# An encoder layer on one core: SBUF tiles moved to addresses that are multiples of 128 bytes

## The chip, the cores and the metric

One core of a Trainium2 chip runs the whole layer. The metric is the device time of one execution in microseconds (us). The kernel before takes 878.75 us, the median of 3 runs (878.52 to 878.77).

## What is computed

One encoder layer on x (512 positions, 1024 channels), all in float32. A projection by `w_in` feeds eight heads of differential attention and a Mamba-2 scan in both directions with 16 heads in 4 groups. The two results, side by side, go through `w_out`; then come a layer norm, SwiGLU (22 column tiles of 128) and a second layer norm:

```
h   = x @ w_in                                  # q, k, v | z, x/B/C, dt
a   = softmax(q1 k1 - |i-j| slope) - lam * softmax(q2 k2 - |i-j| slope)
att = rmsnorm(a @ v) * subln_w * (1 - lambda_init)
ssd = rmsnorm_grouped((scan_fwd + scan_bwd + D x) * silu(z)) * norm_w
x   = layernorm(alpha * x + [att, ssd] @ w_out)
x   = layernorm(alpha * x + (silu(x @ w_gate) * (x @ w_up)) @ w_down)
```

## The kernel before

A float32 product is made of three products in float32r, a float32 format that TensorE takes in one pass. Every operand is split into a high part h and a low part l, and `mm3` (L174 to L179) adds h·h, h·l and l·h. ScalarE makes h by a copy and VectorE makes l by a subtraction (L106 and L107 for the weights). The small products (transposes, attention times v, the scan's products) stay in float32.

```
174    def mm3(o, pairs, first=True, last=True):
177            T.matmul(o, ah, bh, start=first and i == 0, stop=False)
178            T.matmul(o, ah, bl, start=False, stop=False)
179            T.matmul(o, al, bh, start=False, stop=last and i == n - 1)
```

In a matmul the first operand (`ah`) is the stationary one, which the engine loads ahead (LDWEIGHTS, the rows PEld), and the second (`bh`) is the moving one, which streams through, one column of the result for each of its columns. In the profile's names it is out<-moving,stationary: in `wo<-wh,mixl` the weights `wh` move and `mixl` stands.

The stages, in order of time. The first 250 us project B, C, x and z for one scan group after another (`col_units` L181 with 512 moving columns, `row_units` L196 with 256) and run the scan steps of the group before between them (L398 to L518). Then come eight heads of attention (L574 to L645), woven with the next heads' projections q, k (512 columns) and v (256 columns). From about 445 us the output projection runs (`wo`, 512 columns, `outer_units` L650 and `tile_major` L764; the last four weight chunks are kept in tiles `hold`), then the first layer norm. SwiGLU (L946 to L997) multiplies by Winograd's 2 x 2 form: seven products of 256 columns for each column tile, made by `product` (L882 to L889). Two of them take the split weights `wh`, `wl` as the stationary operand, five take sums of weight blocks or a split block (`S1` to `S4`, `A22`), which VectorE makes (L815, L854). The down projection (`dn`, L1006 to L1059) has 512 moving columns again, with the last chunks in tiles `keep` and the last bank in two halves of 256 columns (`dn13`).

The order on each engine is the order of the code with the scheduler's lookahead; nothing in it depends on where a tile lies. A tile's place in SBUF comes from its pool. Pools stack up from the left end, or from the right end with `side="right"`, and every tile's size is rounded up to 32 bytes a partition. So the tiles of 420, 16, 8 and 4 bytes in the first pool (L85 to L90), `msk` with 3920 bytes (L123), and the small tiles of the scan, the heads and the norms push all that lies behind them off any larger grid. The addresses that the program gets, taken modulo 128:

```
 0: cst (with the identity); sx, xd, h, L, yy, gg and the rest of the scan's pool
64: rE, co_B, co_x, co_C, dts, ex, wd, wdp, xraw
96: wr, wh, wl, xh, xl (later x1h, x1l, keep), QS, KS, kl, va, mixh, mixl, msk,
    T1 to T4, lhsC, hid, the ring of split hid tiles (tiles 1 to 9)
32: ss, as, hold, S1 to S4, A22, the resident split hid tiles (10 to 21)
```

Slices within a tile begin at multiples of 128 bytes in all large products but those of `rE`, whose runs are 256 bytes long. The right end of SBUF that the pools are given lies at 96 modulo 128.

Of the kernel before, what the change touches and what calls it, by code (L numbers as in the profile page):

```python
# [8 lines left out]
F32 = mybir.dt.float32  # L9
# [4 lines left out]
P = 128  # L14
NWARM = 2
S = 512
NT = 4
# [25 lines left out]
M_LE, M_GE, M_GT, M_LT, M_ONE, M_HM, M_RM, M_SEL, M_TRI, N_M = 0, 128, 256, 384, 512, 640, 656, 660, 916, 980  # L43
N_C = 1024

V_BIAS, V_ALOG, V_DSK, V_LAM, N_V = 0, 32, 64, 80, 336
P_CW, P_CB, P_SUB, P_NW, N_P = 0, 80, 96, 97, 105
# [3 lines left out]
def encoder(ctx, tc, xt, xs, wall, wdt, consts, masks, vecs, pvec, lnv, out):  # L51
    nc = tc.nc
    V, A, G, T = nc.vector, nc.scalar, nc.gpsimd, nc.tensor
# [19 lines left out]
    def weave(steps, units, counts):  # L73
        """Emits steps in order with counts[i] of the units after step i, and the remaining units at the end."""
        done = 0
        for f, n in zip(steps, counts, strict=True):
            f()
            for u in units[done:done + n]:
                u()
            done += n  # L80
        for u in units[done:]:
            u()

# [1 line left out]
    cst = cp.tile([P, N_C], F32, name="cst")  # L85
    vec = cp.tile([P, N_V], F32, name="vec")
    pv = cp.tile([P, N_P], F32, name="pv")
    mhalf = cp.tile([P, 4], F32, name="mhalf")
    lam = cp.tile([P, 2], F32, name="lam")
    nlam = cp.tile([P, 1], F32, name="nlam")  # L90
    V.memset(mhalf, -0.5)
# [23 lines left out]

# [1 line left out]
    xh = xtp.tile([P, KT, S], R32, tag="xh", name="xh")  # L117
# [4 lines left out]
    ep = eps_.enter_context(tc.tile_pool(name="ep", bufs=1))  # L122
    msk = ep.tile([P, N_M], F32, name="msk")  # L123
    with tc.tile_pool(name="xraw", bufs=1) as xr:
# [56 lines left out]
    def col_units(i, name, done, step=2):  # L181
        """x @ w for 128 columns, transposed: [columns, 512]; then done(psum)."""
        st = {}
# [12 lines left out]
    def row_units(i, name, tag, done):  # L196
        """x @ w for 256 columns: two banks of [128 positions, 2, 256]; done(half, psum)."""
        st = {}
# [16 lines left out]

# [1 line left out]
    sps = ExitStack()  # L217
# [25 lines left out]
    co = {}  # L243
    first_units = conv_units(0, sp, co)

# [1 line left out]
    dtv = ep.tile([P, 2, NT, NH], F32, name="dtv")  # L247
# [4 lines left out]
    sel = msk[:, M_SEL:M_SEL + 256].rearrange("p (a k) -> p a k", a=2)  # L252
    # per direction d: rows erow[d] carry the exponents, the other 64 rows the mask
    erow = (slice(0, 64), slice(64, 128))
# [115 lines left out]

    # stationary parts of the exponents per direction and half of the columns, in the last mix tiles' places
    lhsC = [[mxp[0].tile([P, NT, P], R32, tag=f"m{q}{14 + d}", name=f"lhsC{d}{q}") for q in "hl"] for d in range(2)]
# [6 lines left out]

    # mix^T in two float32r parts: 16 tiles of [128 channels, 512]  # L380
    mixh, mixl = [None] * 16, [None] * 16
# [6 lines left out]

# [1 line left out]
    bc = lambda a, n: a[:, :, None].broadcast_to([a.shape[0], 4, n])  # L390
# [3 lines left out]
    def scan_steps(g):  # L394
        cT, bT, x0, x1 = (co[k, g] for k in ("C", "B", "x0", "x1"))
        sx, H, Ms, yb, gg = {}, {}, {}, {}, {}
        szs = {}
        ssq = sp.tile([P, NT], F32, tag="ssq", name=f"ssq{g}")  # L398
        gs = slice(4 * g, 4 * g + 4)
# [115 lines left out]

# [1 line left out]
    va, qk = {}, {}  # L517
# [31 lines left out]

# [1 line left out]
    late = []  # L551
# [18 lines left out]

# [1 line left out]
    mxp[0] = mxs.enter_context(tc.tile_pool(name="mxa", bufs=1, side="right"))  # L572

    def head_steps(h, ap):  # L574
        QS, KS, kl = qk[h]
        vv, j = va[h // 2], h % 2
        tab = ap.tile([P, 896], F32, tag="tab", name=f"tab{h}")
        mn = ap.tile([P, NT, 2], F32, tag="mn", name=f"mn{h}")
        Z = ap.tile([P, NT, 2], F32, tag="Z", name=f"Z{h}")
        rz = ap.tile([P, NT, 2], F32, tag="rz", name=f"rz{h}")  # L580
        co_ = ap.tile([P, NT], F32, tag="co", name=f"co{h}")
        oq = ap.tile([P, NT], F32, tag="oq", name=f"oq{h}")
        ss, ats, st = {}, {}, {}
# [39 lines left out]
        def fin():  # L623
            f = ap.tile([P, NT], F32, tag="f", name=f"f{h}")
            V.tensor_tensor(f, rz[:, :, 0], rz[:, :, 0], op=ALU.mult)
# [19 lines left out]

# [1 line left out]
    def pair(i, ahead=None):  # L647
        return [w.rearrange("p (k c) -> p k c", k=2) for w in wget(i, ahead)]

    def outer_units(i0, order, lhs, acc, n0, n1, total):  # L650
        """acc(t) += lhs tiles (pairs in order) x weight chunks i0 + n0 .. i0 + n1 - 1."""
        st = {}
# [46 lines left out]

# [1 line left out]
    fx = ctx.enter_context(tc.tile_pool(name="fx", bufs=1))  # L701
# [10 lines left out]
    st6 = fx.tile([P, NT, 4, 6], F32, name="st6")  # L712
    rs = fx.tile([P, NT, 1], F32, name="rs")
    mv = fx.tile([P, NT, 2], F32, name="mv")

# [48 lines left out]
    def tile_major(i0, order, lhs, acc, done, hold, after):  # L764
        """As outer_units, with the last NHELD chunks resident and used one sequence tile at a time."""
        n = len(order)
# [28 lines left out]

# [1 line left out]
    hidp = ctx.enter_context(tc.tile_pool(name="hid", bufs=1, side="right"))  # L797
# [11 lines left out]

    # Winograd's 2 x 2 form: operands from x1^T's blocks B (k half, sequence half)  # L810
    def block(i, j):
# [16 lines left out]
    def t_steps(q):  # L828
        """x1^T of sequence tile 2 + q, and the operands that come of it."""
        b12, b22 = x1t(2 + q, 0), x1t(2 + q, 1)  # L830
# [12 lines left out]

    # operands from the weight blocks of two column tiles: A11 A12 / A21 A22 (columns, k half)
    ops, mats = {}, {}
# [50 lines left out]
    def put(j, f, c, src):  # L896
        """One block of gate (silu) or up (times gate) into hid."""
        d = hid_tile(f)[:, c]
        if j % 2 == 0:
            A.activation(d, src, AF.Silu)  # L900
        else:
            V.tensor_tensor(d, d, src, op=ALU.mult)
# [42 lines left out]

    # the first two tiles of gate and up, whole; sequence half 0 of three chunks first  # L946
    def ff_w(f, w):
# [50 lines left out]

# [1 line left out]
    NEARLY = 1  # L1000
# [5 lines left out]
    def hid_split(e, ph):  # L1006
        """hid tile e in two parts; the later tiles' parts stay for both column halves."""
        key = e if e >= NRING else (ph, e)
# [136 lines left out]
```

## Time and profile before

| | |
|---|---|
| median of 3 runs | 878.75 us |
| span of the profiled execution, first to last instruction | 876.8 us |
| TensorE (PE) busy | 862.4 us, 98% of the span |
| weight loads (PEld) busy | 748.6 us, 85% |
| VectorE (DVE) busy | 616.6 us, 70% |
| ScalarE (ACT) busy | 457.7 us, 52% |
| GpSimd (POOL) busy | 121.3 us, 14% |

The profiled execution's own device time is not given apart from its span; the median of the runs is 1.95 us above the span. In a matmul's row the duration is longer than what it costs, because matmuls are pipelined: the next one starts while the last results still drain. What a matmul costs in a stream is the distance from its start to the next start, called its pitch here. It is read from the timeline.

### The profile page before, as it was taken

How to read it: one execution, taken by the hardware profiler on the slowest of the kernel's cores; microseconds unless marked ns; L12 is line 12 of the kernel's file. 1: busy time of each engine (PE TensorE's matmuls, PEld its weight loads, DVE VectorE, ACT ScalarE, POOL GpSimd, SP SyncE). 2: the span in 40 equal slices, each digit the busy share in tenths (PEclk: the TensorE clock that was granted, in tenths of full speed). 3: DMA queues.
4: the chain of work that ended last, by engine and by line, in shares of the span. 5: the costliest groups of instructions: out<-in, count | busy, mean ns of one | idle time of the engine just before them, and what ended most of it. 6: DMA issues, size and time to landing. Idle time of an engine off the chain costs nothing.

```text
span 876.8 us, 13791 instructions
## 1 busy us (share of the span) xinstructions
PE 862.4 (98%) x5404; PEld 748.6 (85%) x5404; DVE 616.6 (70%) x1071; ACT 457.7 (52%) x893; POOL 121.3 (14%) x137
## 2 busy tenths in 40 slices
PE   7999999999999999999999999999999999999996
PEld 3888989899778687786788889999999999888885
DVE  4978788786567666766644579988888887733617
ACT  4777776667456555655632314555555555621500
POOL 3025252535400000000000023000000000000002
PEclk9999999999999999999999999999999999999999
DMA  7321212112212103111135600343233233332402
GB/s 259 113 96 49 73 50 80 66 49 70 76 49 72 50 25 96 50 49 49 49 109 186 209 25 25 112 129 98 96 123 118 98 116 133 112 96 96 145 1 96
DMA packets 23008, 78.74 MB, mean 90 GB/s; under 512 B 2688, under 2 KB 2944, under 8 KB 22944
## 3 DMA queue, kind: packets, MB, share of 16 engines
q1 hardware_dynamic: 22320, 75.60, 25.8%
q0 software_dynamic: 624, 2.27, 0.8%
q8 instruction: 42, 0.69, 0.3%
q14 instruction: 22, 0.18, 0.1%
HBM read 75.77 MB, written 2.10 MB: 89 GB/s over the span
## 4 chain that ended last, share of the span: by engine, by line
PE 67%; DVE 4%; ACT 1%; issue 1%; DMA 0%; POOLq 0%; POOL 0%; DVEq 0%; ACTq 0%
PE M L887 12%; PE N L887 6%; PE dn L178 4%; PE dn L177 4%; PE dn L179 4%; PE wo L177 3%; PE wo L178 3%; PE wo L179 3%; PE C L887 3%; PE o L618 3%; PE s L592 2%; PE s L590 2%; PE at L606 1%; PE v L177 1%; PE k L177 1%; PE q L177 1%
## 5 line engine op out<-in xcount | busy, mean ns | idle before, releaser
L107 DVE TENSOR_TENSOR wl<-wr,wh 128x1024 fp32r<-128x1024 f32 x101 | 124.5, 1233 | 66.8 <-ACT wh L106 63.5
L106 ACT CAST wh<-wr 128x1024 fp32r<-128x1024 f32 x101 | 105.7, 1049 | 77.6 <-PE wo L179 28.6
L598 ACT ACTIVATE ss<-ss,mn 128x512 f32<-128x512 f32 x64 | 46.0, 720 | 25.9 <-DVE mn L595 25.8
L595 DVE CUSTOM_DVE_ANT_0 ss<-s,tab 128x512 f32<-128x512 f32 x64 | 43.2, 688 | 16.4 <-PE s L592 15.8
L178 PE MATMUL dn<-wl,hidh 128*128 128x512 f32 x130 | 51.0, 392 | 0.0
L177 PE MATMUL dn<-wh,hidh 128*128 128x512 f32 x130 | 50.9, 392 | 0.0
L179 PE MATMUL dn<-wh,hidl 128*128 128x512 f32 x130 | 50.6, 389 | 0.0
L893 ACT COPY e<-M 128x256 f32<-128x256 f32 x60 | 22.4, 372 | 43.1 <-PE M L887 43.0
L456 ACT ACTIVATE rE<-vals,msk 64x128 fp32r<-64x128 f32 x128 | 43.0, 391 | 1.0 <-DVE vals L339 0.4
L177 PE MATMUL wo<-wh,mixh 128*128 128x512 f32 x96 | 38.3, 399 | 0.0
L177 PE MATMUL v<-wh,xh 128*128 128x256 f32 x128 | 37.8, 296 | 0.0
L178 PE MATMUL wo<-wl,mixh 128*128 128x512 f32 x96 | 37.6, 392 | 0.0
L179 PE MATMUL wo<-wh,mixl 128*128 128x512 f32 x96 | 37.5, 390 | 0.0
L179 PE MATMUL v<-wh,xl 128*128 128x256 f32 x128 | 36.7, 286 | 0.0
L177 PE MATMUL z<-wh,xh 128*128 128x256 f32 x128 | 36.4, 286 | 0.0
L178 PE MATMUL v<-wl,xh 128*128 128x256 f32 x128 | 36.3, 284 | 0.0
L179 PE MATMUL z<-wh,xl 128*128 128x256 f32 x128 | 36.2, 283 | 0.0
L178 PE MATMUL z<-wl,xh 128*128 128x256 f32 x128 | 36.2, 283 | 0.0
L618 PE MATMUL o<-va,as 128*128 128x128 f32 x256 | 34.0, 275 | 0.1
L724 POOL TENSOR_TENSOR rs<-rs,mhalf 128x1 f32<-128x1 f32 x8 | 12.2, 1525 | 158.6 <-DVE rs L723 158.6
L708 POOL DMA_DIRECT2D ln<-in_lnv x4 | 2.3, 580 | 227.1 <-PE dn L178 208.8
L618 PEld LDWEIGHTS o<-va,as 128*128 128x128 f32 x256 | 31.6, 192 | 0.7 <-ACT osq L621 0.3
(355 smaller groups left out, 2926.6 us busy)
## 6 DMA issues: line engine op xcount, KB each, us to landing
wr<-in_wall SPq DMA_DIRECT2D x130, 512.0 KB, 3.5
xraw<-in_xt SPq DMA_DIRECT2D x8, 256.0 KB, 6.8
xr<-in_xs SPq DMA_DIRECT2D x4, 512.0 KB, 6.3
ln<-in_lnv POOLq DMA_DIRECT2D x4, 512.0 KB, 4.4
out_y<-xr SPq DMA_DIRECT2D x8, 256.0 KB, 2.0
msk<-in_masks SPq DMA_DIRECT2D x1, 490.0 KB, 5.7
cst<-in_consts SPq DMA_DIRECT2D x1, 448.0 KB, 6.7
vec<-in_vecs POOLq DMA_DIRECT2D x1, 168.0 KB, 5.9
```

The lines of the kernel that those rows point to most:

```text
L106: A.copy(h, raw)
L107: V.tensor_tensor(l, raw, h.bitcast(F32), op=ALU.subtract)
L177: T.matmul(o, ah, bh, start=first and i == 0, stop=False)
L178: T.matmul(o, ah, bl, start=False, stop=False)
L179: T.matmul(o, al, bh, start=False, stop=last and i == n - 1)
L456: A.activation(r[d][e, h], vals[e, sls[t]], AF.Copy, scale=hmask[e, 4 * g + h:4 * g + h + 1])
L590: T.matmul(sbs[c], QS[:, c, sl], KS[:, c], start=True, stop=False)
L595: V.tensor_tensor_reduce(out=s, in0=sb, in1=tab[:, 384 - 128 * t:896 - 128 * t], scale=1.0, scalar=3.0e38, op0=ALU.add, op1=ALU.min, accum ...
L598: A.activation(s, s, AF.Exp, scale=-1.0, bias=mn[:, t, c:c + 1], accum_out=Z[:, t, c:c + 1])
L618: T.matmul(o, ats[t][:, kt * P:(kt + 1) * P], vv[:, kt, j * P:(j + 1) * P], start=kt == 0, stop=kt == NT - 1)
L887: T.matmul(o, x[:, k], y[:, k], start=first and n == 0, stop=last and n == 11, skip_group_check=True)
L893: mats[j]["i" + name] = A.copy(e, src)
```

## The change

The small tiles are merged into few tiles whose sizes are multiples of 128 bytes (`small` with 1792, `msk` with 3968, `sm` with 256 for each head, `rsmv` with 128), the scan's `ssq` moves into spare columns of `msk`, and a tile `top` of 96 bytes is set at the right end. After it every tile that the kernel makes begins at a multiple of 128 bytes.

```diff
-    vec = cp.tile([P, N_V], F32, name="vec")
-    pv = cp.tile([P, N_P], F32, name="pv")
-    mhalf = cp.tile([P, 4], F32, name="mhalf")
-    lam = cp.tile([P, 2], F32, name="lam")
-    nlam = cp.tile([P, 1], F32, name="nlam")
+    small = cp.tile([P, 448], F32, name="small")
+    vec = small[:, 0:N_V]
+    pv = small[:, N_V:N_V + N_P]
+    o_ = N_V + N_P
+    mhalf, lam, nlam = (small[:, o_ + a:o_ + b] for a, b in ((0, 4), (4, 6), (6, 7)))
+    top = ctx.enter_context(tc.tile_pool(name="top", bufs=1, side="right"))
+    top.tile([P, 24], F32, name="top")
...
-    msk = ep.tile([P, N_M], F32, name="msk")
+    mskt = ep.tile([P, 992], F32, name="msk")
+    msk = mskt[:, 0:N_M]
...
-        ssq = sp.tile([P, NT], F32, tag="ssq", name=f"ssq{g}")
+        ssq = mskt[:, N_M + 4 * (g % 2):N_M + 4 * (g % 2) + 4]
...
-        mn = ap.tile([P, NT, 2], F32, tag="mn", name=f"mn{h}")
-        Z = ap.tile([P, NT, 2], F32, tag="Z", name=f"Z{h}")
-        rz = ap.tile([P, NT, 2], F32, tag="rz", name=f"rz{h}")
-        co_ = ap.tile([P, NT], F32, tag="co", name=f"co{h}")
-        oq = ap.tile([P, NT], F32, tag="oq", name=f"oq{h}")
+        sm = ap.tile([P, 64], F32, tag="sm", name=f"sm{h}")
+        mn, Z, rz = (sm[:, 8 * i:8 * i + 8].rearrange("p (t c) -> p t c", c=2) for i in range(3))
+        co_, oq, f = (sm[:, 24 + 4 * i:28 + 4 * i] for i in range(3))
...
-            f = ap.tile([P, NT], F32, tag="f", name=f"f{h}")
...
-    rs = fx.tile([P, NT, 1], F32, name="rs")
-    mv = fx.tile([P, NT, 2], F32, name="mv")
+    rsmv = fx.tile([P, 32], F32, name="rsmv")
+    rs = rsmv[:, 0:NT].rearrange("p (t c) -> p t c", c=1)
+    mv = rsmv[:, NT:3 * NT].rearrange("p (t c) -> p t c", c=2)
```

No instruction is added, removed or moved on any engine; only the tiles' names and addresses differ. One wait is added. On GpSimd, in the heads of attention, the power that ends a head's RMSNorm (L628, on the tile `f`) waits for VectorE before the change:

```order
L628 TENSOR_TENSOR f_3333<-f_3333,mhalf 128x4 [waits DVE_49]
L584 TENSOR_SCALAR tab_3907<-cst 128x896 [waits DVE_49,Pool_49]
L628 TENSOR_TENSOR f_3615<-f_3615,mhalf 128x4 [waits DVE_49]
L584 TENSOR_SCALAR tab_4175<-cst 128x896 [waits DVE_49,Pool_49]
L628 TENSOR_TENSOR f_3870<-f_3870,mhalf 128x4 [waits DVE_49]
```

From the third head on it waits for ScalarE (Activation) too, since `f` now shares the tile `sm` with columns that ScalarE writes:

```order
L629 TENSOR_TENSOR sm_3088<-sm_3088,small 128x4 [waits DVE_49,Activation_49]
L586 TENSOR_SCALAR tab_3878<-cst 128x896 [waits DVE_49,Pool_49]
L629 TENSOR_TENSOR sm_3352<-sm_3352,small 128x4 [waits DVE_49,Activation_49]
L586 TENSOR_SCALAR tab_4141<-cst 128x896 [waits DVE_49,Pool_49]
L629 TENSOR_TENSOR sm_3615<-sm_3615,small 128x4 [waits DVE_49,Activation_49]
```

The instructions and their order are the same; the added wait stands at six of the eight heads.

## Rows read from the trace of the kernel before

**Rows 1.** The page: TensorE's share of the span, and its granted clock in 40 slices.

```profile
PE 862.4 (98%) x5404; PEld 748.6 (85%) x5404; DVE 616.6 (70%) x1071; ACT 457.7 (52%) x893; POOL 121.3 (14%) x137
...
PEclk9999999999999999999999999999999999999999
```

**Rows 2.** Busy time by stage: stretch (us), sum, then each engine with its instructions.

```profile
core 0: us, PE busy (x) PEld busy (x) DVE busy (x) ACT busy (x) POOL busy (x), PEclk, DMA share, GB/s
23.00:250.00 227.00, 226.74 (x1394) 198.67 (x1393) 173.49 (x296) 155.22 (x336) 79.95 (x94) 1.00 0.22 70
250.00:445.00 195.00, 194.87 (x1111) 153.19 (x1110) 131.04 (x303) 112.05 (x259) 12.70 (x13) 1.00 0.17 55
445.00:517.00 72.00, 72.00 (x339) 59.80 (x339) 33.65 (x51) 19.40 (x30) 3.73 (x4) 1.00 0.45 154
562.00:740.00 178.00, 178.00 (x1547) 178.00 (x1546) 153.84 (x239) 100.97 (x167) 0.00 (x0) 1.00 0.34 112
```

**Rows 3.** Timeline of TensorE in SwiGLU: start, duration (us), instruction.

```profile
620.65 0.28 PE L887 MATMUL C<-x1h,wh 128*128 128x256 f32 x1
...
622.09 0.28 PE L887 MATMUL M<-x1h,A22h 128*128 128x256 f32 x1
...
625.94 0.28 PE L887 MATMUL N<-x1l,S3h 128*128 128x256 f32 x1
```

**Rows 4.** Timeline of TensorE in the output projection.

```profile
500.22 0.39 PE L178 MATMUL wo<-wl,mixh 128*128 128x512 f32 x1
...
503.39 0.39 PE L177 MATMUL wo<-holdh,mixh 128*128 128x512 f32 x1
...
505.96 0.39 PE L179 MATMUL wo<-holdh,mixl 128*128 128x512 f32 x1
```

**Rows 5.** Timeline of TensorE at the end of the down projection.

```profile
860.64 0.39 PE L177 MATMUL dn<-keeph,hidh 128*128 128x512 f32 x1
...
863.39 0.28 PE L177 MATMUL dn13x<-keeph,hidh 128*128 128x256 f32 x1
...
868.72 0.28 PE L179 MATMUL dn13ps<-keeph,hidl 128*128 128x256 f32 x1
```

**Rows 6.** Timeline of TensorE: eight transposes, and attention's scores.

```profile
521.08 1.04 PE L740 MATMUL xt<-cst,xr 128*128 128x128 f32 x8
...
321.31 0.50 PE L592 MATMUL s<-kl,QS 64*128 64x512 f32 x2
321.74 0.39 PE L177 MATMUL v<-wh,xh 128*128 128x256 f32 x1
```

**Rows 7.** Groups by line and form: count, then busy us, mean ns, idle before.

```profile
L740 PE MATMUL xt<-cst,xr 128*128 128x128 f32 x32 | 4.3, 272 | 0.0
L887 PE MATMUL C<-x1h,wh 128*128 128x256 f32 x80 | 22.6, 283 | 0.0
L887 PE MATMUL M<-T3h,S3h 128*128 128x256 f32 x80 | 22.2, 277 | 0.4 <-ACT e L893 0.4
L177 PE MATMUL dn<-wh,hidh 128*128 128x512 f32 x130 | 50.9, 392 | 0.0
L177 PE MATMUL v<-wh,xh 128*128 128x256 f32 x128 | 37.8, 296 | 0.0
```

**Rows 8.** Groups by line and form on VectorE: tiles at 96, and tiles at 0.

```profile
L1016 DVE TENSOR_TENSOR hidl<-hid,hidh 128x512 fp32r<-128x512 f32 x32 | 20.5, 684 | 7.6 <-ACT hidh L1015 7.6
L469 DVE TENSOR_TENSOR L<-L,yd 128x512 f32<-128x512 f32 x16 | 10.9, 684 | 2.3 <-PE yd L467 1.1 <-DVE L L468 0.5
```

**Rows 9.** DMA issues: size of one, median us to landing.

```profile
msk<-in_masks SPq DMA_DIRECT2D x1, 490.0 KB, 5.7
cst<-in_consts SPq DMA_DIRECT2D x1, 448.0 KB, 6.7
```

**Rows 10.** Waits of VectorE: us in total, times, longest.

```profile
DVE f L626 <- ACT osq L621: 17.0, 7, 3.6
```

## The prediction

> **What bounds the kernel now.** I read the page first. TensorE is busy for 98% of the span at the full granted clock, 2.4 GHz, in every slice [rows 1]. A busy TensorE need not be the bound, so the second view is the busy time by stage [rows 2]. In SwiGLU (562 to 740 us) TensorE and its weight loads fill all 178.00 us, while VectorE works 153.84 us and ScalarE 100.97 us. In the output projection the other engines are busy for less than half of the 72 us. Behind 445 us TensorE alone sets the time, and every nanosecond taken from a matmul comes off the end. Before 445 us the matmuls also cover nearly all of the time, but VectorE is busy for 173.49 of 227 us and 131.04 of 195 us. There TensorE waits now and then, inside records that look busy.
>
> Since the engine is full, the question is what one matmul costs, and that is its pitch, from the timeline. The reader should divide the distance between two starts by the matmuls between them:
> - SwiGLU, 256 moving columns at address 96 (all modulo 128), stationary tile at 96: from 620.65 to 622.09 twelve matmuls, 0.120 us each. With the stationary tile at 32: from 622.09 to 625.94 thirty-four matmuls, 0.1132 us each [rows 3]. The moving tiles are at 96 in both.
> - Output projection, 512 columns, stationary tile at 96: weights moving at 96 take (503.39 - 500.22) / 14 = 0.2264 us, weights moving at 32 take (505.96 - 503.39) / 11 = 0.2336 us [rows 4]. The stationary tiles are the same.
> - End of the down projection, moving at 96, stationary at 32: (863.39 - 860.64) / 12 = 0.2292 us for 512 columns and (868.72 - 863.39) / 47 = 0.1134 us for 256 [rows 5].
>
> So the pitch does depend on the addresses of both operands, by up to 7 ns, at one clock and with the same work. At 2.4 GHz 256 columns are 106.7 ns and 512 are 213.3 ns, so the excess now is 7 to 13 ns at 256 and 13 to 20 ns at 512.
>
> **What an aligned matmul would cost.** No float32r matmul of before has both operands at a multiple of 128, so I bound it. Below: the columns themselves, 106.7 and 213.3 ns. Above: today's pitch, should nothing change. The nearest rows with a moving tile at 0 are the transposes: eight take 1.04 us, the last one 0.272 us of it, so seven steps of 0.110 us [rows 6, 7]. That is two passes of 128 columns in float32, 106.7 ns plus 3, with stationary tiles that are not at 0. The score products of 64 rows show that 512 columns can pass in 0.215 us: two in 0.43 us [rows 6]; they are at 96 too, but each uses half of the array, so they may overlap. I take 109 and 216 ns, columns plus 2.5 ns.
>
> The Trainium skill gives the same form (TensorE: Matmul & The Clock Gate, section Back-to-back issue gap): warm start-to-start is N / 2.4 plus about 2.5 ns. The transposes agree at 110 ns, and float32r here exceeds it in every row.
>
> **The sum.** No instruction is added or moved, so the gain is a count times a difference of pitches. The counts are those of groups like [rows 7], of one shape in every product:
> - SwiGLU, weights stationary: 6 groups of 80, 480 x (120 - 109) ns = 5.3 us. Sums and A22 stationary: 15 groups of 80, 1200 x 4.3 ns = 5.2 us.
> - Its first two tiles: 144 of 256 columns x 11 ns and 24 of 512 x 13 ns = 1.9 us.
> - Output projection: 288 x (226.5 - 216) ns = 3.0 us, and 96 from `hold` x 17.6 ns = 1.7 us. 96 of the 288 (1.0 us) run before 445 us.
> - Down projection: 462 of 512 columns x about 12 ns = 5.5 us (10.5 with the ring's tiles at 96, 13 with the others), and 132 halves x about 7.5 ns = 1.0 us.
>
> That is 23.6 us, 22.6 of it behind 445 us, where it should come off whole. VectorE in SwiGLU then has its 153.84 us in about 170, 90%, so it does not take over.
>
> Before 445 us: v and z, 768 of 256 columns x 11 ns = 8.4 us; q, k, B, C and x, 768 of 512 x 10.5 ns = 8.1 us; scores 64 x 10.5 ns and the scan's decays 64 x up to 11 ns, 1.3 us; the 1.0 us from above: 18.8 us. How much shows lies between none (another engine's chain sets the pace) and all. I take six tenths, 11.3 us: TensorE is the fullest engine in both stretches, but VectorE and ScalarE follow at 57% to 76% [rows 2], and steps of the scan and of the softmax wait on each other.
>
> **What I cost at nothing.** VectorE and ScalarE do not care: a subtraction of 128x512 takes 684 ns with tiles at 96 and 684 ns with tiles at 0 [rows 8]. DMA: `cst`, already at 0, takes 6.7 us for 448 KB, and `msk` at 96 takes 5.7 us for 490 KB [rows 9]; no gain is visible, and in the start alone, where TensorE waits for x, could a microsecond go either way. The added wait of GpSimd's power on ScalarE: the VectorE step two before it, which reads the sums of squares, waits for ScalarE already, 17.0 us in seven times [rows 10]; behind the power in GpSimd's queue stands only the next head's table, and VectorE waits for the power after that same step. Zero; if ScalarE's awaited write were a later one, at most the longest such wait, 3.6 us, in six heads, and then only if those heads stand on TensorE's path.
>
> Sum: 22.6 + 11.3 = 33.9 us. The pitches come from one execution whose span, 876.8 us, is 1.95 us below the median of 878.75; the difference lies outside the matmuls and stays. **878.75 - 33.9 = 844.9, so 845 us.**
>
> **Rivals.**
> 1. The weight load bounds the 256-column products at 113 ns. For: PEld fills 178.00 of 178 us [rows 2], and the pitch follows the stationary tile's address at 256 columns [rows 3]. Against: the transposes load 128 new columns for each and run at 110 ns. Then the 1200 products gain nothing and the others of 256 columns 7 ns instead of 11: behind 445 us about 3.2 + 1.3 + 3.7 + 5.9 = 14 us, before it (5.1 + 10) x 0.6 = 9 us, together 23: 856 us. Chance 0.22, with every case in which only part of the excess goes. By the skill's estimate (same page, LDWEIGHTS) a load of 128 columns takes P / 1.2, 107 ns, which would leave no such bound above 109.
> 2. The waits of the first half swallow its whole gain, because scan and softmax pace it: 878.75 - 22.6 = 856 us. Against: TensorE is the fullest there. Chance 0.07.
> 3. Addresses on multiples of 32 bytes are as good as any, and the differences in pitch come from what else differs between those products (pools, which engines write near them). For: the 64-row scores at 96 run at 0.215 us [rows 6]. Then nothing changes: 878.75 us. Against: in [rows 3] the moving operand, shape and neighbours are the same. Chance 0.07. The skill would have it so: SBUF — State Buffer, section Specifications, speaks of 16-byte lines with at least two hits needed in each, and contiguous float32 from any multiple of 16 meets that before and after alike.
> 4. Slower: what counts is how the two operands lie to each other, and equal places are the worse. At 256 columns 96 with 96 takes 120 ns and 96 with 32 takes 113.2 [rows 3]. After the change all are equal, so the 1200 products of SwiGLU lose 6.8 ns each and the 72 halves of `dn13` with tiles at 32 too, 8.7 us; the 512-column products with unequal places gain (96 x 7 ns in [rows 4], some 290 x 2.5 ns as in [rows 5]), 1.4 us. That is 886 us. It decides as soon as those 1200 products run at 116 ns or more with the rest unchanged. Against: at 512 columns equal places are the better ones, 226 against 229 and 234 ns [rows 4, 5]. Chance 0.08.
>
> **How the numbers follow.** My forecast has a chance of 0.56: with the front's share anywhere from a third to all, and 1 to 2 ns left on a pitch, it covers 836 to 850. Rivals 1 and 2 (0.29) lie around 856, up to 863 where half of the excess stays. The range 835 to 863 holds both and leaves out rivals 3 and 4. A measurement of this kernel tells about 0.2% (1.8 us) from no change. Faster: 0.56 + 0.29 = 0.85; same: 0.07; slower: 0.08.
>
> **What would show it.** In the changed kernel's timeline the pitch of all SwiGLU products should be one, 109 ns, whether weights or sums stand, and that of `wo`, `hold` and `dn` one, 216 ns. The SwiGLU stage should shrink from 178 to about 168 to 170 us with as many instructions; VectorE's and ScalarE's durations should stay (684 ns). If the 256-column pitch stays at 113 while 512 columns fall to 216, rival 1 holds; if the first 445 us do not shrink although the pitches do, rival 2; if both pitches stay, rival 3; if all 256-column products go to 120, rival 4. I am wrong if 512-column products stay above 225 ns.

## The result: 885.87 us, slower by 0.8%

The changed kernel takes 885.87 us, the median of 4 runs (885.72 to 886.38), against 878.76 us for the kernel before on the same chip (878.52 to 878.78, 4 runs). The ratio is 1.0082, with a 95% interval of 1.0068 to 1.0097. The forecast of 845 us was wrong, and so was its sign; rival 4 named 886 us. The profiled execution has a span of 883.9 us, 7.1 us more than before, the same as the difference of the medians.

One word is used from here on: the **distance** of a product is the address of its stationary operand less that of its moving operand, modulo 256 bytes (why 256, the maps below show). In the SwiGLU stage the kernel before had the weights' products at a distance of 0 and the sums' products at 192: sums at 416 modulo 512, moving tiles at 480. The changed kernel has all of them at 0.

### The profile page after: what moved, and what is told of

It is laid out like the page before. It is cut to its first block, busy times and chain, and to the rows that moved or that the text cites. A ratio compares the mean times of both kernels' runs of the same rounds, so it can differ in the third digit from the quotient of the medians.

```text
span 883.9 us, 13797 instructions
## 1 busy us (share of the span) xinstructions
PE 869.4 (98%) x5404; PEld 756.5 (86%) x5404; DVE 617.1 (70%) x1071; ACT 457.1 (52%) x893; POOL 123.1 (14%) x137
## 4 chain that ended last, share of the span: by engine, by line
PE 67%; DVE 4%; ACT 1%; issue 1%; DMA 0%; POOLq 0%; POOL 0%; DVEq 0%; ACTq 0%
PE M L889 13%; PE N L889 6%; PE dn L181 4%; PE dn L182 4%; PE dn L183 4%; PE wo L181 3%; PE wo L182 3%; PE wo L183 3%; PE C L889 3%; PE o L620 3%; PE s L594 2%; PE s L592 2%; PE at L608 1%; PE v L181 1%; PE k L181 1%; PE q L181 1%
## 5 line engine op out<-in xcount | busy, mean ns | idle before, releaser
L600 ACT ACTIVATE ss<-ss,sm 128x512 f32<-128x512 f32 x64 | 46.0, 719 | 25.7 <-DVE sm L597 25.7
L726 POOL TENSOR_TENSOR rsmv<-rsmv,small 128x1 f32<-128x1 f32 x8 | 12.2, 1527 | 158.0 <-DVE rsmv L725 158.0
```

What stands on the lines that cost most here:

```text
L600: A.activation(s, s, AF.Exp, scale=-1.0, bias=mn[:, t, c:c + 1], accum_out=Z[:, t, c:c + 1])
```

## The profile after

The page of the changed kernel, TensorE's line, for [rows 1]:

```profile
PE 869.4 (98%) x5404; PEld 756.5 (86%) x5404; DVE 617.1 (70%) x1071; ACT 457.1 (52%) x893; POOL 123.1 (14%) x137
```

TensorE has the same 5404 instructions and is busy for 7.0 us more, almost the whole of the loss. VectorE, ScalarE and GpSimd moved by 1.8 us at most. The busy time by stage, for [rows 2] (stretch, sum, then each engine with its instructions, granted clock, DMA share, GB/s):

```profile
23.00:250.00 227.00, 226.72 (x1395) 198.42 (x1394) 173.36 (x296) 155.27 (x336) 81.55 (x94) 1.00 0.21 71
250.00:445.00 195.00, 194.87 (x1112) 153.37 (x1111) 131.23 (x303) 112.25 (x259) 12.77 (x13) 1.00 0.16 55
445.00:517.00 72.00, 72.00 (x340) 60.05 (x339) 33.95 (x53) 19.16 (x29) 4.03 (x5) 1.00 0.43 154
562.00:740.00 178.00, 178.00 (x1485) 178.00 (x1485) 149.34 (x233) 95.92 (x160) 0.00 (x0) 1.00 0.32 107
```

The first three stretches hold one matmul more each: nothing happened up to 517 us. The loss is in the SwiGLU stretch. The same 178.00 us hold 1485 matmuls where they held 1547, so the mean pitch went from 178.00 / 1547 = 115.1 ns to 119.9 ns, at a granted clock of 1.00 (2.4 GHz) as before. TensorE and the weight loads fill the stretch in both. The timeline of TensorE there, for [rows 3]:

```profile
620.74 0.28 PE L889 MATMUL M<-x1h,wh 128*128 128x256 f32 x1
...
623.62 0.28 PE L889 MATMUL M<-x1h,A22h 128*128 128x256 f32 x1
...
626.50 0.28 PE L889 MATMUL N<-x1h,S3h 128*128 128x256 f32 x1
```

From 620.74 to 623.62 there are 24 products with the weights standing, 0.1200 us each, as before. From 623.62 to 626.50 there are 24 with `A22` and `S1` standing: 0.1200 us too, where they took 0.1132. The output projection, for [rows 4], and the end of the down projection, for [rows 5]:

```profile
499.77 0.39 PE L181 MATMUL wo<-wh,mixh 128*128 128x512 f32 x1
...
503.17 0.39 PE L181 MATMUL wo<-holdh,mixh 128*128 128x512 f32 x1
...
506.57 0.39 PE L181 MATMUL wo<-holdh,mixh 128*128 128x512 f32 x1
```

```profile
865.81 0.39 PE L181 MATMUL dn<-keeph,hidh 128*128 128x512 f32 x1
...
869.89 0.28 PE L181 MATMUL dn13x<-keeph,hidh 128*128 128x256 f32 x1
...
875.28 0.28 PE L181 MATMUL dn13ps<-keeph,hidh 128*128 128x256 f32 x1
```

With 512 columns, weights `wh` and `hold` take the same now: (503.17 - 499.77) / 15 = 0.2267 us and (506.57 - 503.17) / 15 = 0.2267 us; `hold` took 0.2336. `dn` takes (869.89 - 865.81) / 18 = 0.2267, where it took 0.2292. The halves of 256 columns went the other way: (875.28 - 869.89) / 45 = 0.1198, where they took 0.1134. So equal places cost 120 ns at 256 columns and 226.7 ns at 512, whether both lie at 96 or at 0 modulo 128.

The account, from these pitches and counts: 1200 sums' products x 6.7 ns = 8.0 us lost, 71 halves x 6.6 ns = 0.5 us lost, 96 products from `hold` x 6.9 ns = 0.7 us and 252 of `dn` x 2.5 ns = 0.6 us won. That makes 7.2 us; 7.1 us were measured. By the starts of the same products in the two traces the four are 7.66 and 0.45 us lost, 0.58 and 0.46 us won, 7.07 us in all.

## The experiments

### One pad of 64 bytes in the changed kernel

```diff
     fp = ffs.enter_context(tc.tile_pool(name="fp", bufs=2))
+    fp.tile([P, 16], F32, tag="fpad", name="fpad", bufs=1)
```

This moves what lies in the pool of the sums, `A22` and the sums first of all, to a distance of 64; no other pool moves.

> The changed kernel with one pad of 64 bytes at the head of SwiGLU's pool, so that the stationary sums S1 to S4 and A22 lie at 64 modulo 128 while the moving tiles stay at 0. Theory A (what counts is how the stationary and the moving tile lie to each other): the 1200 products of the sums go back from 120 to 113 ns, the span falls by about 8 us and the time is 877 to 879 us. Theory B (the stationary tile's own place counts, 32 was good and 0 and 96 are bad): 64 was never seen with float32r, so it could be anything, 120 if only 32 is good: 886 us. Theory C (something else in the merged tiles made the change slower): 886 us.

Measured: 883.36 us (883.22 to 883.89), ratio 1.0050 (1.0033 to 1.0067). The stretch from 562 to 740 us holds 1506 matmuls:

```profile
562.00:740.00 178.00, 178.00 (x1506) 178.00 (x1505) 151.30 (x235) 96.94 (x161) 0.00 (x0) 1.00 0.32 110
```

The sums' products run at a mean of 117.8 ns, neither the 113 nor the 120 that the theories had. A distance of 64 is better than equal places, and not as good as the 192 of the kernel before. The distance modulo 128 can't be all.

### Many places at once in the full kernel

Two kernels gave the sums another place in each column tile, in steps of 4 to 16 bytes, and each of the four held chunks of `wo` its own place (a longer tile, and a view into it). `e` has 4 places instead of 5, for room. The first of the two; the second has steps of 16 bytes and longer pads:

```diff
+    tp_.tile([P, 16], F32, tag="tpad", name="tpad", bufs=1)
...
-        h, l = (fp.tile([P, n], R32, tag=tag + q, name=f"{names[0]}{q}_{j}", bufs=bufs) for q in "hl")
+        o = {2: 0, 3: 2, 4: 4, 5: 6, 6: 8, 7: 10, 8: 12, 9: 14, 10: 16, 11: 18, 12: 20, 13: 22, 14: 24, 15: 26, 16: 28, 17: 30, 18: 1, 19: 3, 20: 5, 21: 7}.get(j, 0)
+        h, l = (fp.tile([P, n + 32], R32, tag=tag + q, name=f"{names[0]}{q}_{j}", bufs=bufs)[:, o:o + n] for q in "hl")
```

> A map of the pitch in one run: the changed kernel, the stationary sums of column tile j moved by 0, 8, 16 ... 120 bytes (j from 2 to 17; then 4, 12, 20, 28), the moving tiles T1 to T3 moved by 64 bytes against x1, and the four resident weight chunks of the output projection (moving) by 16, 32, 64 and 96 bytes; one buffer fewer for the evacuated products, to make room. Theory A: the pitch is a function of the difference of the two addresses alone: products with x1 and products with T show the same curve, shifted by 64 bytes; 120 ns at difference 0, 113 at 64, and somewhere between or beyond a value near 109. Theory B: the products with x1 and with T agree at the same stationary address. For 512 columns theory A expects 233 or 229 ns at a difference of 64 and 226.5 at 0.

> The same map farther out: the sums moved by 192 + 0, 16 ... 96 bytes, T1 to T3 by 192 bytes the other way, so that the differences are 192 to 288 bytes for x1 and 384 to 480 for T; the resident chunks of the output projection moved by 48, 80, 112 and 8 bytes. Theory A with a period of 128 bytes: 256 and 384 look like 0 (120 ns), 192 and 448 like 64 (113 ns). With a longer period they differ, which would show that the grid is not 128 bytes.

Measured: 884.15 and 884.17 us, one run each. The sums' pitch had a mean of 118.1 and 118.2 ns, and the curve that was to separate the theories didn't show. Two faults of the design: the pad at the head of the moving tiles' pool didn't move them, since on the right stack the pool's start moves down by the pad's size; and the longer tiles put the low part of a sum at another distance than the high part, so no column tile had one distance. For 512 columns they did say something: `hold`, its high part moved by 8 to 112 bytes, took a median of 229 to 234 ns over twelve products, never the 226.7 of equal places. Inconclusive for 256 columns.

### A map of the pitch by itself

The next kernel does nothing but the triples of products, on four tiles of real data, so that the place of each operand is free:

```
def product(n, mv, st):
    """12 matmuls of n columns: moving tiles at byte mv, stationary tiles at byte st (h, l, four k)."""
    o = banks[nb[0] % 4][:, 0:n]
    nb[0] += 1
    a, b = mv // 4, st // 4
    for k in range(4):
        mh, ml = (x[:, 512 * k + a:512 * k + a + n] for x in (MH, ML))
        sh, sl = (x[:, 128 * k + b:128 * k + b + 128] for x in (SH, SL))
        T.matmul(o, sh, mh, start=k == 0, stop=False)
        T.matmul(o, sh, ml, start=False, stop=False)
        T.matmul(o, sl, mh, start=False, stop=k == 3)
```

> This kernel leaves out the encoder altogether: it loads four tiles (a moving and a stationary matrix, each in its high and low part, at equal places modulo 512) and runs the kernel's triple of products (high by high, high by low, low by high, twelve to a bank) at 16 x 16 places of the two operands in steps of 32 bytes, 24 products of 256 columns at each, then at 4 x 16 places with 512 columns; what it writes out is not the encoder's result. Theory A (what counts is the distance of the two operands modulo 128): the pitch of 256 columns is 120 ns on the diagonal, where the distance is 0, about 113 to 118 wherever it is 64, the same for every place of the moving operand; distances of +64 and -64 modulo 512 give the same. Theory B (the absolute place of the moving operand counts, 96 modulo 128 being good): the pitch depends on the row of the map alone: 113 at 96 modulo 128, 118 to 120 at 0. Theory C (the distance counts modulo 256 or 512): 113 at distances of 448 modulo 512 (the kernel before) and 118 at 64 (the run with the 64-byte pad). Theory D (the prediction's forecast, that multiples of 128 are best for each operand): 109 where both are at 0. For 512 columns A expects 227 on the diagonal and 229 to 234 off it, D 216 at 0.

Measured: the mean pitch in ns of the last 18 of 24 products at a place, from their starts in the trace; each line takes all places with that distance (32 places for 256 columns, 8 for 512):

```
distance        0      32      64      96     128     160     192     224
256 columns 119.8   118.1   117.9   117.2   118.4   120.2   117.7   118.3   (median)
            119.7   118.1   113.6   117.2   118.3   119.8   117.6   116.7   (lowest)
            120.2   118.3   118.0   120.2   118.9   120.2   117.8   118.3   (highest)
512 columns 227.2   233.2   233.4   234.0   233.4   233.6   228.9   232.9   (median)
```

Most places of one distance agree, wherever the moving operand lies (14 of the 256 are more than 1 ns off their median): theories B and D are out. Distances that are the same modulo 256 agree, those that are the same modulo 128 don't (0 and 128). With 512 columns equal places are the best of these. With 256 columns they are among the worst, yet nothing at a distance of 192 runs at the 113.3 ns that the kernel before has there. But four places at a distance of 64 run at 113.6, while the 28 others at that distance run at 117.9. One distance with two pitches. The place just before is at a distance of 32 in nearly all 32 cases, the four among them, and the four have the moving operand at 128 with the stationary at 192, or 224 with 32, modulo 256. So it is what went before, farther back, or the places themselves; the next map tells.

### The way in, and the two undo runs

The second map enters each place as the kernel before does, from products at equal places. The two kernels beside it are the undo from both sides. One is the changed kernel with a pad of 448 bytes, which is 192 modulo 256: what lies in the pool of the sums is 64 bytes below the moving tiles again, and every other pool stays where the change put it. The other is the kernel before with a pad that gives the sums equal places, and no other edit.

```diff
     fp = ffs.enter_context(tc.tile_pool(name="fp", bufs=2))
+    fp.tile([P, 112], F32, tag="fpad", name="fpad", bufs=1)    # in the changed kernel
...
     fp = ffs.enter_context(tc.tile_pool(name="fp", bufs=2))
+    fp.tile([P, 16], F32, tag="fpad", name="fpad", bufs=1)     # in the kernel before
```

> Leaves out the encoder as the first map did (same four tiles, same triple of products); now each place is entered from a run of products whose operands lie at equal places (120 ns each), as the sums' products are in the SwiGLU stage: 24 of those, then 24 at the place measured, for distances of 0 to 496 in steps of 16 bytes at three places of the moving operand; then the same entered from 512-column products, runs of 96 at distances of 64, 192, 320 and 448, and 512-column products alone at distances of 0 to 224. Theory A (the distance modulo 256 alone sets the pitch, as most of the first map says: 119.7, 118.2, 117.8, 117.2, 118.7, 120.1, 117.8, 117.8 for 0 to 224 in steps of 32): these values again, whatever went before. Theory E (two steady rhythms exist at a distance of 64 or 192, one of 113.4 and one of 117.8, and what went before picks one; the first map has 113.5 in five of its cells, all at a distance of 64): entered from equal places, a distance of 192 (the kernel before: 448 modulo 512) gives 113, a distance of 64 (the run with the 64-byte pad) 117 to 118, and each stays for all 96 products; entered from another rhythm they can come out the other way round.

> The changed kernel with a pad of 448 bytes instead of 64 at the head of the sums' pool: everything stays at a multiple of 128 but the sums and A22, which lie 64 bytes below the moving tiles modulo 512, as they do in the kernel before; no other tile moves against the changed kernel. If the distance, sign included, is what the change undid: sums' products back at 113.3 ns, 1200 x 6.7 = 8.0 us off 885.9: 877 to 879. If only the absolute places matter (multiples of 128 are worse): 883 to 884, as with the 64-byte pad.

> The kernel before with one line added: a 64-byte tile at the head of the sums' pool, so that the sums and A22 lie at 480 modulo 512 like the moving tiles; none of the change's merging, and no tile at a multiple of 128. If the distance of the two operands is the whole of it: the sums' products go from 113.3 to 120.0 ns and the kernel from 878.8 to 886 to 887. If the multiples of 128, the merged tiles or the other DMAs make the change's loss: 878 to 879.

(The first map has four such places, not the five that the expectation speaks of.) The timeline of the second map, where two runs of 96 products each come out of 12 at equal places:

```profile
674.69 0.28 PE L77 MATMUL b<-MH,SH 128*128 128x256 f32 x1
...
686.00 0.28 PE L77 MATMUL b<-MH,SH 128*128 128x256 f32 x1
...
687.44 0.28 PE L77 MATMUL b<-MH,SH 128*128 128x256 f32 x1
...
698.32 0.28 PE L77 MATMUL b<-MH,SH 128*128 128x256 f32 x1
```

At a distance of 64 (674.69 to 686.00) a product takes 11.31 / 96 = 0.1178 us; at equal places (686.00 to 687.44) 1.44 / 12 = 0.1200; at 192 (687.44 to 698.32) 10.88 / 96 = 0.1133. Each keeps its pitch for all 96. All six places tried at a distance of 192 (448 modulo 512 among them) ran at 113.3 or 113.4 when entered from equal places, and all six at 64 ran at 117.8 or 117.9. Entered from 512-column products at equal places, 192 gave 117.6 or 117.7, at addresses that had given 113.3: it is what went before, not the places. That is theory E: at these distances there are two steady rhythms, and the entry picks one. The distance of what went before isn't all of the entry either: with the moving operand going from 96 to 64, a run at 64 behind a run at 64 took 113.6, and a run at 192 behind one at 192 took 117.8.

The undo in the changed kernel: 878.19 us (877.83 to 878.64, 10 runs), ratio 0.9990 (0.9981 to 1.0000). Its SwiGLU stretch holds 1547 matmuls again:

```profile
562.00:740.00 178.00, 178.00 (x1547) 178.00 (x1546) 153.89 (x239) 101.51 (x169) 0.00 (x0) 1.00 0.32 110
```

And its timeline there, with both rhythms side by side:

```profile
618.52 0.28 PE L890 MATMUL M<-x1h,wh 128*128 128x256 f32 x1
...
621.40 0.28 PE L890 MATMUL M<-x1h,A22h 128*128 128x256 f32 x1
...
623.78 0.28 PE L890 MATMUL M<-T2h,S1h 128*128 128x256 f32 x1
```

24 weights' products take 2.88 us, 0.1200 each; the 21 that follow take 2.38 us, 0.1133 each. The kernel before with its sums at equal places takes 886.38 us (886.08 to 886.58, 4 runs), ratio 1.0085 (1.0070 to 1.0100), and its stretch holds 1486 matmuls:

```profile
562.00:740.00 178.00, 178.00 (x1486) 178.00 (x1484) 149.32 (x231) 94.80 (x160) 0.00 (x0) 1.00 0.30 107
```

So the distance of the sums' products, each block of them entered from the weights' products at equal places, is the cause, shown from both sides. One line of 64 bytes in the kernel before, without a single merged tile, costs what the whole change costs. And the change with that one distance put back is as fast as before, with all its merged tiles, its DMAs and its added wait in place.

### Finer steps, mixed distances and stalls

The third map adds a place for each of the four tiles and a stall, in which ScalarE still reads the bank that the next product wants.

```diff
-    def product(n, mv, st):
+    def product(n, mv, st, ml_=None, sl_=None):
...
+    def stall():
+        for i in range(4):
+            A.copy(sink, banks[i])
```

> Leaves out the encoder as the two maps did (same tiles, same triple of products). First distances around 192, 0 and 64 in steps of 4 bytes; then the high and the low stationary tile at different distances; then the low moving tile moved alone; then 512 columns in steps of 16; last, products of 256 columns entered from a stall, in which the bank is still being read by ScalarE. Theory E (two rhythms at distances of 64 and 192; the one of 113 is picked when such a place is entered from products at equal places) expects 113 at 192 alone and over 116 four bytes to either side, 512 columns lowest at equal places (226.7), and after a stall at a distance of 192 either rhythm: 113 for some of the runs, 118 for others. Theory F (any narrow distance can have a rhythm that the steps of 16 missed) expects 256-column products at 109 to 113 somewhere among the steps of 4 or the mixed distances. If after a stall the products at 192 keep 117.8, a kernel with all its products at that distance would win 2 ns and not 7 on each that is at 120 now.

Measured: entered from equal places, 4 bytes beside 192 the pitch is 118 to 119 (188) and 118 (196), as E expects. No distance and no mixture went below 113.3, so theory F's 109 is not there. But 113.3 isn't tied to 192 alone: distances of 52 and 76 settle there after some products, and so do the mixtures of a high part at 192 with a low part at 64 and the other way round. With 512 columns 16, 144 and 240 equal the 226.7 of equal places and nothing is below. After a stall, the six runs at 64 all settled at 113.3, and the seven at 192 went either way: 113.3 after the three idle times of 1.35 us, 117.8 after the four of 1.41 to 1.50 us. Two of these, with TensorE's idle time ahead of the first product in brackets:

```profile
713.69 0.39 PE L78 MATMUL b<-MH,SH 128*128 128x256 f32 x1 [1.46 <-ACT sink L90]
...
714.15 0.28 PE L78 MATMUL b<-MH,SH 128*128 128x256 f32 x1
...
714.86 0.28 PE L78 MATMUL b<-MH,SH 128*128 128x256 f32 x1
...
718.13 0.38 PE L78 MATMUL b<-MH,SH 128*128 128x256 f32 x1 [1.35 <-ACT sink L90]
...
718.58 0.28 PE L78 MATMUL b<-MH,SH 128*128 128x256 f32 x1
...
719.26 0.28 PE L78 MATMUL b<-MH,SH 128*128 128x256 f32 x1
```

Six products lie between the second and the third row of each. After an idle time of 1.46 us they take (714.86 - 714.15) / 6 = 0.118 us, after 1.35 us (719.26 - 718.58) / 6 = 0.113, at the same distance of 192.

### Versions that should beat both

If all the products of the SwiGLU stage ran at 113.3, its 624 weights' products would win 4.2 us. Three kernels try it, the first two with three pads each (for x, for the moving sums, for the stationary sums), the third with one pad and by views that move x1 alone; to make room, `e` has 4 places instead of 5 there:

```diff
+    pad = ctx.enter_context(tc.tile_pool(name="pad", bufs=1))
+    pad.tile([P, 16], F32, name="xpad")        # 48 in the second
     xtp = ctx.enter_context(tc.tile_pool(name="xtp", bufs=1))
...
     hidp = ctx.enter_context(tc.tile_pool(name="hid", bufs=1, side="right"))
+    hidp.tile([P, 48], F32, name="hpad")       # 16 in the second and third
...
+    fp.tile([P, 48], F32, tag="fpad", name="fpad", bufs=1)     # 16 in the second
...
-    x1h = xtp.tile([P, KT, S], R32, tag="xh", name="x1h")      # the third, and x1l alike
+    x1h = xtp.tile([P, KT * S + 64], R32, tag="xh", name="x1h")[:, 48:48 + KT * S].rearrange("p (k s) -> p k s", k=KT)
```

> The changed kernel with three pads, so that in the SwiGLU stage every product of 256 columns, those of the weights too, has its stationary operand 64 bytes below the moving one (a distance of 192 modulo 256): 64 bytes ahead of x's tiles, 192 at the head of hid's pool and 192 at the head of the sums' pool. The first map's rule (two rhythms at 192) gives two ends: the rhythm of 113 everywhere: 624 weight products go from 120 to 113.3, 4.2 us off 878.2, 874.0; or, since no run of equal places comes before any more and a stall leaves either rhythm, 117.8 everywhere: 1200 x 4.5 less 624 x 2.2 = 4.0 us on, 882.2. Before that stage z and v go to a distance of 64 (113 or 118 for 120) and the 512-column projections to 192 (229 for 227), which is lost or won only where PE sets the pace there.

> The same with x's tiles 192 bytes further, hid's pool 64 and the sums' pool 64: every product of 256 columns in the SwiGLU stage at a distance of +64. In the third map each product run at 64 that came out of a stall settled at 113, and those that came from equal places at 117.8. With the rhythm of 113: 874 in that stage's terms, and on top of it 0 to 5 us lost by the 512-column projections and the held chunks, which now lie at 64 (233.5 for 226.7; 768 of them ahead of the SwiGLU stage, 168 held): 874 to 880. With 117.8: 882 to 888.

> Only x1 (not x) and the sums' moving tiles moved 64 bytes down, by views into tiles that are 256 bytes longer, so that the SwiGLU stage's 256-column products lie at +64 and nothing else changes its distance; to make room the ring of copied-out products has 4 places instead of 5. With the rhythm of 113 after the stall that opens the stage: 1824 products at 113.3, 878.2 less 4.2 = 874.0; with 117.8: 882. A lost ring place may add up to 2 us.

All at 192: 881.51 us (880.82 to 882.47, 6 runs), ratio 1.0028 (1.0016 to 1.0040). The rhythm of 117.8 took nearly the whole stage, the second of the two ends named; no run of equal places comes before a product there any more:

```profile
562.00:740.00 178.00, 178.00 (x1514) 178.00 (x1513) 150.83 (x235) 97.78 (x164) 0.00 (x0) 1.00 0.32 108
```

Only behind its 24 products of 512 columns the other rhythm is there for 48 products, and a wait of TensorE for ScalarE ends it:

```profile
550.89 0.28 PE L893 MATMUL M<-x1h,wh 128*128 128x256 f32 x1
...
556.21 0.28 PE L893 MATMUL N<-T1h,S1l 128*128 128x256 f32 x1
557.27 0.38 PE L893 MATMUL M<-T3h,S3h 128*128 128x256 f32 x1 [0.78 <-ACT e L899]
...
557.73 0.28 PE L893 MATMUL M<-T3h,S3h 128*128 128x256 f32 x1
...
558.79 0.28 PE L893 MATMUL M<-x1h,wh 128*128 128x256 f32 x1
```

Ahead of the wait 47 products take 5.32 us, 0.1132 each; behind it 9 take 1.06, 0.1178 each. The time of this kernel isn't the stage's alone: against the changed kernel, by the starts in the traces, `dn`, most of whose products lie at 64 now, takes 2.0 us more, and the products before 445 us 1.7 us less.

All at 64, x with them: ten runs, six of them from 876.78 to 877.14, three from 883.98 to 884.05, one at 880.90; the ratio of the medians is 1.0001 (0.9978 to 1.0023). The granted clock doesn't tell them apart: it is 0.995 in a run of 884.01 and in one of 876.78. The profiled execution is one of the 884. Its stage opens at 117.8; it has gone over to 113.3 when the timeline shows the rhythm turn back, at a wait of TensorE for VectorE's `x1l`:

```profile
535.59 0.28 PE L183 MATMUL ff<-x1h,wh 128*128 128x256 f32 x1
...
537.29 0.28 PE L183 MATMUL ff<-x1h,wh 128*128 128x256 f32 x1
...
539.11 0.38 PE L184 MATMUL ff<-x1l,wh 128*128 128x256 f32 x1 [1.20 <-DVE x1l L751]
...
539.45 0.28 PE L183 MATMUL ff<-x1h,wh 128*128 128x256 f32 x1
...
540.87 0.28 PE L183 MATMUL ff<-x1h,wh 128*128 128x256 f32 x1
```

Ahead of the wait 15 products take 1.70 us, 0.1133 each; behind it 12 take 1.42, 0.118 each, and the rest of the stage keeps 117.8. With x1 alone moved the same wait, also 1.20 us, leaves the fast rhythm, in the profiled execution of the third kernel:

```profile
538.69 0.38 PE L182 MATMUL ff<-x1l,wh 128*128 128x256 f32 x1 [1.20 <-DVE x1l L749]
...
539.02 0.28 PE L181 MATMUL ff<-x1h,wh 128*128 128x256 f32 x1
...
540.38 0.28 PE L181 MATMUL ff<-x1h,wh 128*128 128x256 f32 x1
```

That is 1.36 us for 12 products, 0.1133 each. This kernel takes 875.70 us (875.45 to 876.37, 5 runs), ratio 0.9965 (0.9952 to 0.9978), and beats both. It falls 1.7 us short of 874.0, of which its own pad was to be 1 us: 198 products of `dn` had come to a distance of 192. They ran at 233.3 ns from 754 to 768 us and at 228.9 from 808 to 826 us, where the kernel before has 0.2292 us [rows 5] and the first map 228.9 ns at that distance; so at 512 columns, too, one distance had two pitches. The last run moves them back to equal places:

```diff
+    rpad = ctx.enter_context(tc.tile_pool(name="rpad", bufs=1, side="right"))
+    rpad.tile([P, 48], F32, name="rpad")
     dnr = ctx.enter_context(tc.tile_pool(name="dnr", bufs=1, side="right"))
```

> The run before with a pad of 192 bytes ahead of the down projection's ring of split tiles, which the 64 bytes of hid's pool had put at a distance of 192: the ring's 198 products of 512 columns go from about 232 to 227 ns, 1.0 us. If the SwiGLU stage keeps its rhythm of 113 as in the five runs before, 874.5 to 875; a run near 882 would say that the rhythm at 64 does not always catch.

Measured: 875.25 us, ratio 0.9974 (0.9956 to 0.9991); of 12 runs ten lie from 874.80 to 875.85 and two at 882.25 and 882.29. The pad brought 0.45 us by the medians; by the starts in the traces `dn` takes 0.6 us less. The profiled execution, at 875.05, holds as many matmuls in the stretch as the run before, 113.2 ns each:

```profile
562.00:740.00 178.00, 178.00 (x1573) 178.00 (x1572) 156.29 (x243) 102.37 (x171) 0.00 (x0) 1.00 0.34 115
```

The two at 882 lie 7.0 us above the median. That is the size of the slow rhythm: the stage's 1824 products of 256 columns take 217.3 us in the profiled run of 884 us above and 210.1 us here, by their starts. No profile of such a run of this kernel was taken, so it is argued, not shown. The rhythm at 64 doesn't always catch. The kernel before is 3.5 us slower than the good runs, but it has the more robust form: its 120 ns products at equal places lead each block of sums into the rhythm of 113, and the run that restored this showed all ten executions within 0.8 us.

## Why the prediction was wrong, point by point

- **TensorE is the bound, and behind 445 us every nanosecond of pitch comes off or goes on.** Right, with the sign turned: 7.0 us more of TensorE's busy time, 7.1 us more in the span.
- **"What an aligned matmul would cost"** is the step that failed. It took 109 and 216 ns from float32 transposes and 64-row scores, as the price of an operand that begins at a multiple of 128. There is no such price: with both operands at multiples of 128 the products took 120.0 ns at 256 columns and 226.7 at 512. In both maps the place of the moving operand by itself doesn't set the pitch; the distance between the two does, together with what ran before. The transposes still step by some 110 ns, as in [rows 6]; they were never a sample of what a float32r triple does. [Rows 3] alone held the better reading: two products with the moving operand at 96, the one at equal places the slower. The forecast wrote this down, as rival 4, and gave it 0.08, because at 512 columns equal places are the better ones. The first map shows that both hold: 227.2 of up to 234.0 at 512 columns, 119.8 of 117.2 to 120.2 at 256. A rule from one shape didn't carry over to the other.
- **The gap of 2.5 ns** (the Trainium skill, TensorE: Matmul & The Clock Gate, Back-to-back issue gap) was used as support for 109 ns. That section calls it the gap of an isolated matmul, and says that in a stream with a weight load to each matmul both set the spacing; the products here are such a stream. At no distance tried did float32r products of 256 columns run steadily below 113.3 ns. For these products the measurement decides.
- **The sum.** Each term was a count times a pitch. The counts stand (1200, 480, 144, 96). The terms themselves were: sums 5.2 us won, in fact 8.0 lost; weights' products 5.3 us won, in fact none; the first two tiles 1.9 us won, in fact none; `hold` 1.7 us won, in fact 0.7; `dn` 5.5 us won, in fact 0.6; its halves 1.0 us won, in fact 0.5 lost; `wo` 3.0 us won, in fact none.
- **Before 445 us** 11.3 us were to come. No pitch changed there (x and the weights lay at equal places before and do after), so nothing did. Six tenths was never put to the test.
- **What was costed at nothing** held. VectorE's subtraction takes 685 ns [rows 8] (684 before), the two DMAs land in 5.4 and 6.6 us where they took 5.7 and 6.7 [rows 9], and the wait for the sums of squares is 17.1 us in seven times where it was 17.0 [rows 10]:

```profile
L1018 DVE TENSOR_TENSOR hidl<-hid,hidh 128x512 fp32r<-128x512 f32 x32 | 20.6, 685 | 7.5 <-ACT hidh L1017 7.5
```

```profile
DVE sm L627 <- ACT osq L623: 17.1, 7, 3.6
```

- **Rival 4** was right in mechanism, price and place: 120 ns for all 256-column products, 886 us, with some 290 `dn` products where 252 gained. What it lacked is that unequal is not good in itself. With the pad of 64 bytes the sums are unequal too, and took 117.8.
- **Rivals 1 to 3** fall as forecasts: rival 1 wanted 512 columns at 216 (226.7; whether the weight load has a part in the pitch of 256 columns no run settles), rival 2 a gain behind 445 us, rival 3 no change of any pitch. Rival 3 had a rule of 16-byte lines beside it (the Trainium skill, SBUF — State Buffer, Specifications). In the third map the distances 176, 192 and 208, all multiples of 16, take 118.1, 113.3 and 116.7 ns, and 200, which is none, 116.7: such lines don't order them.
- **Range and chances.** 835 to 863 left out the one case that came. With the evidence of [rows 3] a slower result deserved a chance at least as large as that of the forecast's 109 ns, for which no float32r row of the trace spoke.

## What to carry to other kernels

Alignment of a tile by itself bought nothing here; what a stream of matmuls pays depends on how the stationary and the moving tile lie to each other and on what ran before, and the sign can differ between 256 and 512 columns. So read the pitch from the timeline for each pair of tiles, list it by distance, and treat an edit of any small tile below them as an edit of that distance. Before forecasting a price that no row shows, let the nearest rows of the same operand type speak first: here those of 256 columns said that equal places were the slow ones.

## What the runs showed that was not expected

- At one distance, one shape and one clock (1.00) the same stream of float32r products of 256 columns runs steadily at 113.3 or at 117.8 ns, for runs of 24 and 96 in the maps and for nearly a whole stage of 1824 in the kernel, and a stall of TensorE can turn the one into the other. It makes a kernel's time fall into two groups 7 us apart (876.8 to 877.1 and 884.0 in ten runs of one program).
- A distance of 192 modulo 256, entered from equal places, gave 113.3 in every place tried; a distance of 64 entered so gave 117.8, and 113.3 after each stall of the map.
- Why a distance has the rhythm it has, and why 0.78 and 1.20 us of waiting turned it in two programs and 1.20 us did not in a third, stays open. The runs show where and when, not what inside the engine or the memory does it.
